# Attention's output projection in seven half products: where its weight sums are kept, in which order the products run, and how far ahead the factors are loaded

## The chip, the core and the metric

The kernel runs on one core of a Trainium2 chip. The core has five engines that run side by side, each with its own instruction queue in order: TensorE (PE, matmuls, with PEld for loading the stationary operand), VectorE (DVE), ScalarE (ACT), GpSimd (POOL) and SyncE (SP). SP issues nearly all plain loads from memory; POOL issues those that add to what already lies in the tile. Engines wait for each other on semaphores. The metric is the device time of one execution in microseconds, lower is better; the time before is the median of 3 runs, 1007.43 us (1006.94 to 1008.52).

## What is computed

A decoder trunk of two layers, one sequence of 512 tokens, width 1024, everything in float32. Layer 0 mixes tokens by causal pooling, layer 1 by attention with three groups of heads (windows of 128, 512 and 2048 with dilations 1, 4, 16). Both layers end in a SwiGLU block.

```python
for i in range(DEPTH):
    h = rmsnorm(x, norm_mix[i])
    if i % N_MIXERS == 0:
        y = pool_mixer(h, pool_w_in[j], pool_w_group[j], pool_scale[j], pool_w_out[j])
    else:
        y = attn_mixer(h, attn_w_qkv[j], attn_w_out[j])
    x = x + y
    h = rmsnorm(x, norm_ffn[i])
    x = x + swiglu(h, ffn_w_gate[i], ffn_w_up[i], ffn_w_down[i])
return rmsnorm(x, norm_final)
```

The last step of `attn_mixer` is what matters here. Each head's output is scaled by its group's share, the 16 heads are put side by side (`merged`, 512 x 1024), and the result is multiplied by `attn_w_out` (1024 x 1024):

```python
merged = jnp.concatenate(
    [o_g * (N_ATTN_GROUPS * alpha[:, :, g]).astype(o_g.dtype)[:, :, None, None] for g, o_g in enumerate(outs)],
    axis=2,
).reshape(B, S, D_ATTN)
return jnp.einsum('bse,ed->bsd', merged, w_out)
```

## The kernel before

**Precision.** Every float32 matrix is split in two parts, `hi` (a cast to fp32r) and `lo` (the rest, `x - hi`), and a product is three matmuls: hi*hi, hi*lo, lo*hi. A weight tile of 128 x 1024 thus costs one cast on ACT (line 179) and one subtraction on DVE (line 183).

**The stream of weights.** All weight tiles stand in one list, `queue`, in the order of use. `weights(i)` (line 157) does three things: it loads tiles up to `load_ahead` places on (an item's own `ahead` overrides it), it splits loaded tiles up to `split_ahead` places on, and it hands out item `i`. Raw tiles come from the pool `wraw` (5), split ones from the ring `wspl` (5 pairs) or, for items with `"pool": "b"`, from a second pool that is open only for a while. `held` says how many ring tiles are in use elsewhere. An item with `"sums"` takes its raw tile from `pools["s"]`, and loading stops at such an item while that pool isn't open (line 161). An item with `"cast_behind"` has its cast put behind a named instruction on ACT.

**Order.** PE runs in program order. On the other engines a planner orders the instructions before the run by priority, its own costs and due times; `tc.high_priority(URGENT)` puts a block ahead, `tc.issue_after(ins)` puts it behind an instruction on the same engine. At run time each engine keeps the planned order.

**Seven half products.** Attention's output projection multiplies the merged matrix by the weight in the manner of Strassen and Winograd: with both cut in quarters, seven products take the place of eight. `SEVEN_OUT = (False, True)` uses it for attention only; layer 0 runs the plain `out_projection`. Each product has a left operand (a quarter or a sum of quarters of the merged matrix, split to hi and lo by `Left`) and a right operand, two weight items z = 0, 1 (`enqueue_seven`, line 207). Products 0, 3 and 6 use a plain quarter of the weight; 4 adds a second block by DMA; product 1's item is a sum in a tile of its own (the `sraw` of the trace: a base by SP, a second block added by POOL). Products 2 and 5 use that same tile after one more block each is added to it (`loads`, line 188), which can only be issued after the split of the item before. The products accumulate in three pairs of PSUM banks: `accs = {0: p, 1: r, 2: p, 3: q, 4: p, 5: r, 6: p}`; after each, `flush` adds the banks into the residual stream `x` on DVE.

The order before is 0, 1, 2, 5, 4, 3, 6. `seven_projection` (line 554) runs it: 24 matmuls a product (line 571), and between products the left splits (`left.behind`), the squares and gains of the norm, and before product 6 the transposes of the first two blocks of rows (`turned_rows`). `left.reserve` takes a ring tile for the left operand `u4`.

**What comes ahead of it.** After the scores and the value projection, the group shares go through a small DMA to memory (`far`) and come back as factors, spread over the partitions (`weights_of`, line 1434, two POOL DMAs each). `merged(t)` (line 1521) makes two heads' output on PE in one of 4 PSUM banks (`mm`), and DVE multiplies it by factor `t` into a raw tile (lines 1538 and 1542). Five factors are loaded ahead, into `LB0` to `LB2` and the halves of `even_rows`; the other three follow as tiles come free. Along with it `Left.first` and `Left.second` make the first left operands. The raw tiles are parts of `pT`, the transposed scores.

`angles` holds the cosines and sines of the rotary embedding, `odd_rows` rows of the norm; `masks` the score masks, in the tile that the norm's `gain` takes later.

Of the kernel before, what the change touches and what calls it, by code (L numbers as in the profile page):

```python
# [17 lines left out]
P = 128  # L18
# [52 lines left out]
SEVEN = (0, 1, 2, 5, 4, 3, 6)  # L71
# [7 lines left out]
def trunk_kernel(ctx: ExitStack, tc: tile.TileContext, x_in, xT, gam, gains, consts, ident_d, w0, wT, w1, wv, w_down, out):  # L79
# [49 lines left out]
    def load(i):  # L129
# [3 lines left out]
        if item.get("sums"):  # L133
            raw = pools["s"].tile([P, 1024], F32, name="sraw")
        else:
            raw = (pools["v"] if item["kind"] == "v" else wraw).tile([P, 1024], F32, name="vraw" if item["kind"] == "v" else "wraw")
# [20 lines left out]
    def weights(i, split_ahead=4, load_ahead=5, held=0):  # L157

        load_ahead = queue[i].get("ahead", load_ahead)
        for n in range(loaded["w"], min(len(queue), i + load_ahead)):  # L160
# [5 lines left out]
        load_sums()  # L166
        while len(ready) < min(loaded["w"], i + split_ahead):
# [36 lines left out]
    j_in.append([enqueue(w0[i], (2, S)) for i in range(4, 8)])  # L204
    w_out, wo = (rows_of(wT[i]) for i in range(2))

    def enqueue_seven(w, order, then=None):
# [295 lines left out]
    class Left:  # L503
# [6 lines left out]
        def split(self, u, src, ks=(slice(0, 4),)):  # L510
            hi, lo = self.places[u]
            for k in ks:
                split(hi[:, k, :], lo[:, k, :], src[:, k, :])
# [33 lines left out]
        def reserve(self):  # L547

            if 4 not in self.places:
                self.places[4] = [  # L550
                    wspl.tile([P, 1024], F32R, name=name).rearrange("p (k s) -> p k s", k=4) for name in ("whi", "wlo")
                ]

    def seven_projection(js, left, norm, shift, p, r, q, tps, after_first, keep):
# [8 lines left out]
        def products(i, ws, ts=range(2)):  # L563
            hi, lo = left.places[(0, 1, 2, 3, 6, 5, 4)[i]]
            places = [(z, t, c) for z in range(2) for t in ts for c in range(2)]
# [16 lines left out]
        def product(i):  # L582
            products(i, operands(i))
# [16 lines left out]
        product(5)  # L600
# [24 lines left out]
    with ExitStack() as pctx:  # L625
# [4 lines left out]
        if SEVEN_OUT[0]:  # L630
            raw = [pm.tile([P, 4, S], F32, name=f"raw{i}") for i in range(2)]
            spare_sum = pm.tile([P, 4, 256], F32, name="spare_sum")
        p_hi, p_lo = (pm.tile([P, NC, S], F32R, name=name) for name in ("p_hi", "p_lo"))
# [53 lines left out]
        for k in range(2):  # L687
# [3 lines left out]
            if k == 0:  # L691
                nc.vector.tensor_sub(bands_lo, bands[:, :, :HEAD], bands_hi[:, k, :, :HEAD].bitcast(F32))
        v, s, r = (tmp.tile([P, 4], F32, name=name) for name in ("v4", "s4", "r4"))
# [36 lines left out]
        def group_products(half, banks):  # L730
            whi, wlo = weights(j_grp[half])
            for gg in range(2):
                g = 3 - (2 * half + gg)
                for m in range(2):
# [7 lines left out]
                    if SEVEN_OUT[0]:  # L742
                        with tc.high_priority(URGENT):
                            nc.scalar.activation(raw[half][:, 2 * gg + m, :], ps, AF.Copy, scale=sc)
# [6 lines left out]
                    )  # L751

# [19 lines left out]
        if SEVEN_OUT[0]:  # L772
            pools["s"] = open_pool("pools", 2)
            p, r = ([mm.tile() for _ in range(2)] for _ in range(2))

            def after_first():
                group_products(1, early)
# [396 lines left out]
    with ExitStack() as actx:  # L1174
# [8 lines left out]
        angles = aw.tile([P, D], F32, name="angles", bufs=1)  # L1183
# [183 lines left out]

        ring = [ap.tile([P, S], F32, name=f"LB{g}") for g in range(3)]
# [133 lines left out]
        seven = SEVEN_OUT[1]  # L1502
        pools["b"] = actx.enter_context(tc.tile_pool(name="wob", bufs=3 if seven else 4, reuse_waits="tile"))
        if seven:
            pools["s"] = actx.enter_context(tc.tile_pool(name="wos", bufs=2, reuse_waits="tile"))
        two = mp.tile([P, D], F32, name="even_rows")
        of_heads = [weights_of(t, to) for t, to in enumerate(ring + [two[:, cs] for cs in COLS])]
        m_hi, m_lo = h_hi, h_lo
        if seven:
# [5 lines left out]
            places.update({6: places[0], 3: places[1]})  # L1515
            left = Left(raw, fours(flat_p, 8 * S, 256), places)
# [4 lines left out]
        def merged(t):  # L1521
# [14 lines left out]
            with tc.high_priority(URGENT):  # L1536
                if t < 3:
                    nc.vector.tensor_mul(o, ps, of_heads.pop(0))
                    of_heads.append(weights_of(5 + t, ring[t]))
# [104 lines left out]
```

## Time and profile before

| | |
|---|---|
| median of 3 runs | 1007.43 us |
| the profiled execution | 1007.74 us |
| its span | 1006.0 us |
| PE busy | 975.3 us, 97% |
| DVE busy | 800.7 us, 80% |
| ACT busy | 583.6 us, 58% |
| POOL busy | 134.8 us, 13% |
| read from memory | 165.09 MB |

The span is the time from the first to the last instruction; the profiled execution's own time is 1.7 us longer. A line of a group or of a timeline names the engine, the line of the kernel, the operation, the tile written and the tiles read, and, in brackets, how long the engine was idle before it and who ended that. A line of waits has the total, the number and the longest. A line of windows gives the busy time (and the number of instructions) of PE, PEld, DVE, ACT and POOL in a stretch, then the granted clock of TensorE (1.00 is full), the share of the DMA engines, and GB/s. Where a helper makes all instructions of a kind, they have one line, so the names of the tiles tell them apart: `sraw` is product 1's sum, `bhi` and `blo` are splits in the second pool, `sc`, `mm` and `tp` are PSUM banks.

### The profile page before, as it was taken

How to read it: one execution, taken by the hardware profiler on the slowest of the kernel's cores; microseconds unless marked ns; L12 is line 12 of the kernel's file. 1: busy time of each engine (PE TensorE's matmuls, PEld its weight loads, DVE VectorE, ACT ScalarE, POOL GpSimd, SP SyncE). 2: the span in 40 equal slices, each digit the busy share in tenths (PEclk: the TensorE clock that was granted, in tenths of full speed). 3: DMA queues.
4: the chain of work that ended last, by engine and by line, in shares of the span. 5: the costliest groups of instructions: out<-in, count | busy, mean ns of one | idle time of the engine just before them, and what ended most of it. 6: DMA issues, size and time to landing. Idle time of an engine off the chain costs nothing. (4 is left out here: it accounts for less than half of the span.)

```text
span 1006.0 us, 15591 instructions
## 1 busy us (share of the span) xinstructions
PE 975.3 (97%) x6004; PEld 863.5 (86%) x6004; DVE 800.7 (80%) x1099; ACT 583.6 (58%) x909; POOL 134.8 (13%) x132
## 2 busy tenths in 40 slices
PE   9999999999999999999999986879999999999997
PEld 7888899988988998898888985669998898899886
DVE  6475799888897888688976528789989788888877
ACT  5573666656755767474534614567655566566655
POOL 0002010111012101102121141011101101111110
PEclk9999999999999999999999997889999999999999
DMA  8557276589469866652222295586747966887652
GB/s 323 185 175 181 46 216 169 140 208 239 125 175 253 211 179 147 159 194 91 84 61 66 85 234 103 152 190 186 190 126 202 246 166 148 225 240 174 157 123 118
DMA packets 82186, 168.24 MB, mean 167 GB/s; under 512 B 6256, under 2 KB 6640, under 8 KB 82112
## 3 DMA queue, kind: packets, MB, share of 16 engines
q1 hardware_dynamic: 59088, 123.09, 37.2%
q0 software_dynamic: 22736, 43.89, 25.5%
q8 instruction: 47, 0.77, 0.3%
q10 hardware_dynamic: 288, 0.27, 0.1%
q14 instruction: 27, 0.22, 0.1%
HBM read 165.09 MB, written 2.13 MB: 166 GB/s over the span
## 5 line engine op out<-in xcount | busy, mean ns | idle before, releaser
L183 DVE TENSOR_TENSOR wlo<-wraw,whi 128x1024 fp32r<-128x1024 f32 (+2 forms) x190 | 221.8, 1172 | 59.7 <-ACT whi L179 59.0
L179 ACT CAST whi<-wraw 128x1024 fp32r<-128x1024 f32 (+2 forms) x189 | 183.9, 979 | 129.9 <-PE pair L888 28.0
L179 ACT CAST whi<-vraw 128x1024 fp32r<-128x1024 f32 (+1 forms) x108 | 105.1, 979 | 120.4 <-DVE vraw L185 40.7
L183 DVE TENSOR_TENSOR wlo<-vraw,whi 128x1024 fp32r<-128x1024 f32 (+1 forms) x108 | 121.5, 1133 | 47.1 <-ACT whi L179 47.0
L888 PE MATMUL pair<-h,whi 128*128 128x512 f32 (+1 forms) x640 | 143.2, 349 | 0.0
L888 PEld LDWEIGHTS pair<-h,whi 128*128 128x128 f32 x640 | 109.1, 189 | 13.4
L888 PE MATMUL pair<-t,whi 128*128 128x512 f32 (+1 forms) x512 | 110.6, 337 | 0.0
L1032 PE MATMUL pair<-whi,u_hi 128*128 128x512 f32 (+1 forms) x284 | 109.9, 387 | 0.0
L1032 PE MATMUL pair<-wlo,u_hi 128*128 128x512 f32 (+1 forms) x284 | 109.9, 387 | 0.0
L1032 PE MATMUL pair<-whi,u_lo 128*128 128x512 f32 (+1 forms) x284 | 109.7, 386 | 0.0
L888 PEld LDWEIGHTS pair<-t,whi 128*128 128x128 f32 x512 | 86.0, 190 | 8.4
L888 PE MATMUL pair<-h,wlo 128*128 128x256 f32 x512 | 89.2, 281 | 0.0
L888 PEld LDWEIGHTS pair<-h,wlo 128*128 128x128 f32 x512 | 76.1, 188 | 4.2
L144 POOL DMA_DIRECT2D wraw<-w x22 | 26.6, 1209 | 388.0 <-DMA wraw<-w 112.7
L185 DVE TENSOR_TENSOR vraw<-vraw,wraw 128x1024 f32<-128x1024 f32 (+1 forms) x66 | 75.2, 1139 | 0.6
L888 PE MATMUL pair<-t,wlo 128*128 128x256 f32 x384 | 71.9, 282 | 0.0
L299 PE MATMUL mm<-h,whi 128*128 128x512 f32 (+1 forms) x176 | 64.3, 365 | 0.0
L301 PE MATMUL mm<-h,wlo 128*128 128x512 f32 (+1 forms) x176 | 63.4, 360 | 0.0
L300 PE MATMUL mm<-h,whi 128*128 128x512 f32 (+1 forms) x176 | 63.4, 360 | 0.0
L1032 PEld LDWEIGHTS pair<-whi,u_lo 128*128 128x128 f32 x284 | 53.3, 188 | 10.7
L1032 PEld LDWEIGHTS pair<-whi,u_hi 128*128 128x128 f32 x284 | 53.4, 188 | 10.4
L1032 PEld LDWEIGHTS pair<-wlo,u_hi 128*128 128x128 f32 x284 | 53.4, 188 | 10.3
(399 smaller groups left out, 2053.3 us busy)
## 6 DMA issues: line engine op xcount, KB each, us to landing
wraw<-w SPq DMA_DIRECT2D x116, 512.0 KB, 4.4
wraw<-w_down SPq DMA_DIRECT2D x32, 512.0 KB, 4.1
vraw<-w SPq DMA_DIRECT2D x22, 512.0 KB, 4.6
wraw<-w POOLq DMA_DIRECT2D x22, 512.0 KB, 7.6
vraw<-w POOLq DMA_DIRECT2D x22, 512.0 KB, 8.9
wraw<-wT SPq DMA_DIRECT2D x16, 512.0 KB, 4.7
vraw<-w_down POOLq DMA_DIRECT2D x12, 512.0 KB, 6.6
wraw<-w_down SPq DMA_DIRECT2D x24, 256.0 KB, 3.2
```

What stands on the lines that cost most here:

```text
L144: nc.gpsimd.dma_start(dst, more, accum_op=ALU.add)
L179: nc.scalar.copy(hi[:, :n], raw[:, :n])
L183: nc.vector.tensor_sub(lo[:, :n], raw[:, :n], hi[:, :n].bitcast(F32))
L185: nc.vector.tensor_add(raws[into][:, :n], raws[into][:, :n], raws[more][:, :n])
L299: nc.tensor.matmul(ps, lhsT=whi, rhs=xhi, start=first, stop=False, **kw)
L300: nc.tensor.matmul(ps, lhsT=whi, rhs=xlo, start=False, stop=False, **kw)
L301: nc.tensor.matmul(ps, lhsT=wlo, rhs=xhi, start=False, stop=last, **kw)
L888: mat = lambda o, w, m, **kw: nc.tensor.matmul(o, lhsT=w, rhs=m, skip_group_check=True, **kw)
L1032: nc.tensor.matmul(acc(t), lhsT=u, rhs=w, start=first, stop=n == len(places) - 1, skip_group_check=True)
```

## The change

Eight edits, most of them in the attention layer:

1. The sums' raw tiles: instead of a pool of two tiles that opens after the scores, `pools["s"]` gives `odd_rows` and `angles`, and it is there from the end of the loop over queries and keys. `angles` moves to the pool that lives through the whole layer.
2. Only products from the third in the order on put their second half in pool `b`; both halves of products 0 and 1 take ring tiles.
3. The order is 0, 1, 2, 4, 5, 3, 6.
4. Product 2's two casts are tied behind the casts of the left operands 1 and 2.
5. `Left.behind`: the splits for 5, 6, 3 and 4 leave the urgent block and stand behind other products; `u4` has its own tile (`reserve` is gone).
6. In `seven_projection` the squares and gains stand elsewhere, product 5's weights are asked for ahead of them, and product 6 is cut so that the transposes stand between its first and second half of block 0.
7. Six factors ahead: `masks` takes the sixth.
8. In layer 0, the last input weight has `ahead` 8, and the second group's weights are asked for with `split_ahead` 1.

The parts under `SEVEN_OUT[0]` (sums and ties in the pooling layer) aren't run, as that flag is off.

```diff
-SEVEN = (0, 1, 2, 5, 4, 3, 6)
+SEVEN = (0, 1, 2, 4, 5, 3, 6)
...
-            raw = pools["s"].tile([P, 1024], F32, name="sraw")
+            raw = pools["s"]()
...
+    def load_until(end):
+
+        for n in range(loaded["w"], min(len(queue), end)):
             if queue[n].get("sums") and "s" not in pools:
                 break
             if queue[n]["kind"] == "w":
                 load(n)
             loaded["w"] = n + 1
         load_sums()
...
-    j_in.append([enqueue(w0[i], (2, S)) for i in range(4, 8)])
+    j_in.append([enqueue(w0[i], (2, S), **({"ahead": 8} if i == 7 else {})) for i in range(4, 8)])
...
-                item = dict(kind="w" if src else "sum", shape=(2, S), rows=True, ahead=8, **({"pool": "b"} if z else {}))
+                item = dict(kind="w" if src else "sum", shape=(2, S), rows=True, ahead=8, **({"pool": "b"} if z and i > 1 else {}))
...
-            with tc.high_priority(URGENT):
-                if i is None:
+            if i is None:
+                with tc.high_priority(URGENT):
                     self.next_sum(FIRST)
                     self.split(2, self.spare)
-                    self.split(5, more[:, :, FIRST])
-                    nc.vector.tensor_sub(t[:, :, FIRST], more[:, :, FIRST], t[:, :, FIRST])
-                elif i == 0:
-                    self.split(6, t[:, :, FIRST])
-                elif i == 1:
-                    self.split(3, more[:, :, SECOND])
-                    self.next_sum(SECOND)
-                elif i == 4:
-                    self.split(4, self.spare)
+            elif i == 0:
+                nc.vector.tensor_sub(t[:, :, FIRST], more[:, :, FIRST], t[:, :, FIRST])
+                self.split(6, t[:, :, FIRST])
+            elif i == 1:
+                self.split(5, more[:, :, FIRST])
+                self.next_sum(SECOND)
+            elif i == 2:
+                self.split(3, more[:, :, SECOND])
+                self.split(4, self.spare)
...
-            return [weights(j, split_ahead=6, held=z + (i in (4, 3, 6))) for z, j in enumerate(js[i])]
+            return [weights(j, split_ahead=6, held=z) for z, j in enumerate(js[i])]
...
         product(1)
         product(2)
-        product(5)
+        product(4)
+        ws = operands(5)
+        for b in range(2):
+            norm.square(b, 1)
+            norm.gained(b, 1)
+        product(5, ws)
         for b in range(2):
             norm.square(b, 0)
             norm.gained(b, 0)
-        left.reserve()
-        product(4)
-        for b in range(2):
-            norm.square(b, 1)
-            norm.gained(b, 1)
             norm.prepare(b)
         product(3)
         for t in range(2):
             norm.square(2 + t, 0, q[t])
-        rests = turned_rows(norm, shift, list(enumerate(tps())))
         ws = operands(6)
-        rests()
+        products(6, ws, (0,), (0,))
+        turned_rows(norm, shift, list(enumerate(tps())))()
+        products(6, ws, (0,), (1,))
         for t in range(2):
+            if t:
+                products(6, ws, (1,))
             norm.gained(2 + t, 0)
-            products(6, ws, (t,))
             flush(6, t)
...
-            whi, wlo = weights(j_grp[half])
+            whi, wlo = weights(j_grp[half], 1 if half else 4)
...
-        angles = aw.tile([P, D], F32, name="angles", bufs=1)
+        seven = SEVEN_OUT[1]
+        angles = (ap if seven else aw).tile([P, D], F32, name="angles", bufs=1)
...
+        if seven:
+            free = [odd_rows, angles]
+            pools["s"] = lambda: free.pop(0)
...
-        if seven:
-            pools["s"] = actx.enter_context(tc.tile_pool(name="wos", bufs=2, reuse_waits="tile"))
-        two = mp.tile([P, D], F32, name="even_rows")
-        of_heads = [weights_of(t, to) for t, to in enumerate(ring + [two[:, cs] for cs in COLS])]
+        two = mp.tile([P, D], F32, name="even_rows")
+        factors = ring + [two[:, cs] for cs in COLS]
+        if seven:
+            factors.append(masks[:, :S])
+        of_heads = [weights_of(t, to) for t, to in enumerate(factors)]
...
+            places[4] = [mp.tile([P, 4, 256], F32R, name=name) for name in ("u4_hi", "u4_lo")]
...
-                    of_heads.append(weights_of(5 + t, ring[t]))
+                    if len(factors) + t < 8:
+                        of_heads.append(weights_of(len(factors) + t, ring[t]))
...
                     elif t == 4:
                         left.second()
+                        queue[j_wo[2][0]]["cast_behind"] = left.cast.ins
                     elif t == 7:
                         left.behind(None)
+                        queue[j_wo[2][1]]["cast_behind"] = left.cast.ins
```

More of the change, by code (lines that the diff above doesn't have):

```diff
@@ L155, in load_sums @@
                 done.append(i)
-    def weights(i, split_ahead=4, load_ahead=5, held=0):
-        load_ahead = queue[i].get("ahead", load_ahead)
-        for n in range(loaded["w"], min(len(queue), i + load_ahead)):
+    def load_until(end):
+        for n in range(loaded["w"], min(len(queue), end)):
             if queue[n].get("sums") and "s" not in pools:
@@ L166, in weights @@
         load_sums()
+    def weights(i, split_ahead=4, load_ahead=5, held=0):
+        load_ahead = queue[i].get("ahead", load_ahead)
+        load_until(i + load_ahead)
         while len(ready) < min(loaded["w"], i + split_ahead):
@@ L512, in split @@
             for k in ks:
-                split(hi[:, k, :], lo[:, k, :], src[:, k, :])
+                self.cast = split(hi[:, k, :], lo[:, k, :], src[:, k, :])[0]
         def first(self, k):
@@ L532, in behind @@
             t, more = self.raw
-            with tc.high_priority(URGENT):
-                if i is None:
+            if i is None:
+                with tc.high_priority(URGENT):
                     self.next_sum(FIRST)
                     self.split(2, self.spare)
-                    self.split(5, more[:, :, FIRST])
-                    nc.vector.tensor_sub(t[:, :, FIRST], more[:, :, FIRST], t[:, :, FIRST])
-                elif i == 0:
-                    self.split(6, t[:, :, FIRST])
-                elif i == 1:
-                    self.split(3, more[:, :, SECOND])
-                    self.next_sum(SECOND)
-                elif i == 4:
-                    self.split(4, self.spare)
[L547 to L552, printed above, removed]
+            elif i == 0:
[7 more added lines that the diff above has]
+                self.split(4, self.spare)
     def seven_projection(js, left, norm, shift, p, r, q, tps, after_first, keep):
@@ L560, in operands, with products @@
         def operands(i):
-            return [weights(j, split_ahead=6, held=z + (i in (4, 3, 6))) for z, j in enumerate(js[i])]
-        def products(i, ws, ts=range(2)):
+            return [weights(j, split_ahead=6, held=z) for z, j in enumerate(js[i])]
+        def products(i, ws, ts=range(2), zs=range(2)):
             hi, lo = left.places[(0, 1, 2, 3, 6, 5, 4)[i]]
-            places = [(z, t, c) for z in range(2) for t in ts for c in range(2)]
+            places = [(z, t, c) for z in zs for t in ts for c in range(2)]
             for z, t, c in places:
@@ L580, in flush, with product @@
                     nc.vector.tensor_sub(at, at, accs[i][t])
-        def product(i):
-            products(i, operands(i))
+        def product(i, ws=None):
+            products(i, ws or operands(i))
             for t in range(2):
@@ L632, in trunk_kernel @@
             spare_sum = pm.tile([P, 4, 256], F32, name="spare_sum")
+            sums = [pm.tile([P, 1024], F32, name=f"sum{i}") for i in range(2)]
         p_hi, p_lo = (pm.tile([P, NC, S], F32R, name=name) for name in ("p_hi", "p_lo"))
@@ L692, in trunk_kernel @@
                 nc.vector.tensor_sub(bands_lo, bands[:, :, :HEAD], bands_hi[:, k, :, :HEAD].bitcast(F32))
+        if SEVEN_OUT[0]:
+            pools["s"] = lambda: sums.pop(0)
+            load_until(j_out[1][-1] + 1)
         v, s, r = (tmp.tile([P, 4], F32, name=name) for name in ("v4", "s4", "r4"))
@@ L743, in group_products @@
                         with tc.high_priority(URGENT):
-                            nc.scalar.activation(raw[half][:, 2 * gg + m, :], ps, AF.Copy, scale=sc)
+                            made = nc.scalar.activation(raw[half][:, 2 * gg + m, :], ps, AF.Copy, scale=sc)
                             if half == 0 and m == 1:
@@ L751, in group_products @@
                     )
+            return SEVEN_OUT[0] and made
         quarters = lambda t: t.rearrange("p a b -> p (a b)").rearrange("p (u k s) -> p u k s", u=4, k=4)
@@ L772, in trunk_kernel @@
         if SEVEN_OUT[0]:
-            pools["s"] = open_pool("pools", 2)
             p, r = ([mm.tile() for _ in range(2)] for _ in range(2))
             def after_first():
-                group_products(1, early)
+                made = group_products(1, early)
+                for i in (2, 5):
+                    for j in j_out[i]:
+                        queue[j]["cast_behind"] = made.ins
                 left.second()
```

1 line of the change is left out of this document (removed).

## The prediction

> **What bounds the kernel now.** I read the page first, then the windows over the attention layer's end, who waited for whom there, and last the order of time on ACT, DVE, POOL and SP.
>
> ```profile
> span 1006.0 us, 15591 instructions
> ...
> PE 975.3 (97%) x6004; PEld 863.5 (86%) x6004; DVE 800.7 (80%) x1099; ACT 583.6 (58%) x909; POOL 134.8 (13%) x132
> ```
>
> TensorE is the bound: idle for 1006.0 - 975.3 = 30.7 us in all, and no edit here removes a matmul. So a gain can only come from that idle time and the slow clock behind it. Most lies in one place (windows: PE, PEld, DVE, ACT, POOL busy with counts, then PE clock, DMA share, GB/s):
>
> ```profile
> core 0: us, PE busy (x) PEld busy (x) DVE busy (x) ACT busy (x) POOL busy (x), PEclk, DMA share, GB/s
> 594.07:601.57 7.50, 7.43 (x132) 7.18 (x132) 3.13 (x5) 0.34 (x2) 6.69 (x11) 1.00 0.79 236
> 601.57:609.92 8.35, 0.00 (x1) 0.00 (x1) 2.48 (x4) 2.33 (x3) 3.00 (x5) 0.73 0.94 205
> 609.92:625.91 15.99, 15.99 (x81) 13.15 (x81) 15.35 (x16) 6.26 (x8) 2.80 (x4) 0.82 0.48 83
> 625.91:631.39 5.48, 0.00 (x1) 0.00 (x0) 4.97 (x7) 1.90 (x2) 0.00 (x0) 0.81 0.00 0
> 631.39:668.00 36.61, 33.17 (x151) 25.93 (x151) 28.19 (x46) 22.69 (x35) 6.06 (x5) 0.89 0.73 184
> 680.05:720.35 40.30, 40.30 (x339) 40.09 (x337) 40.28 (x55) 26.66 (x38) 4.84 (x4) 1.00 0.71 183
> 594.07:722.30 128.23, 105.97 (x764) 95.24 (x765) 106.13 (x148) 69.87 (x102) 24.59 (x29) 0.91 0.68 166
> PE mm L1532 <- DVE pT L1538: 8.4, 1, 8.4
> PE sc L571 <- DVE wlo L183: 5.5, 1, 5.5
> PE pair L914 <- ACT keep L966: 2.0, 1, 2.0
> PE mm L401 <- ACT even_rows L387: 1.9, 1, 1.9
> ```
>
> Between the merged heads' first matmul (594.07) and the FFN's wait that ends at 722.30, PE idles 128.23 - 105.97 = 22.3 us; 8.4 and 5.5 of it are two single waits. The same rows warn: DVE is busy 15.35 of 15.99, 4.97 of 5.48 and 40.28 of 40.30 us. Wherever PE stops waiting, DVE is nearly full.
>
> The first wait is a blocked head of a queue:
>
> ```profile
> 584.69 1.07 SPq L142 DMA_DIRECT2D sraw<-wT  x2
> 593.01 3.14 POOL L1438 DMA_DIRECT2D LB<-far  x6 [7.96 <-DMA far<-ropea]
> 598.32 2.54 POOL L144 DMA_DIRECT2D sraw<-wT  x2
> 606.36 1.04 ACT L179 CAST whi<-sraw 128x1024 fp32r<-128x1024 f32 x1 [11.94 <-DMA sraw<-wT]
> 607.44 1.23 DVE L183 TENSOR_TENSOR wlo<-sraw,whi 128x1024 fp32r<-128x1024 f32 x1 [8.46 <-ACT whi L179]
> 609.18 0.68 DVE L1538 TENSOR_TENSOR pT<-mm,LB 128x512 f32<-128x512 f32 x1
> ```
>
> Product 1's weight sum has its base at 584.69, but its adding DMA stands on POOL behind the factors (598.32), so ACT casts it only at 606.36. DVE stands in order before its rest (8.46 us idle), and behind that is the third multiply, which frees the PSUM bank that PE waits for.
>
> The second wait has two parts:
>
> ```profile
> 630.12 1.22 DVE L183 TENSOR_TENSOR wlo<-sraw,whi 128x1024 fp32r<-128x1024 f32 x1
> 631.26 1.22 DVE L183 TENSOR_TENSOR blo<-sraw,bhi 128x1024 fp32r<-128x1024 f32 x1
> 631.96 1.22 POOL L188 DMA_DIRECT2D sraw<-wT  x1 [10.79 <-DVE wlo L183]
> 637.82 1.06 ACT L179 CAST whi<-sraw 128x1024 fp32r<-128x1024 f32 x1 [10.01 <-DMA sraw<-wT]
> 638.91 1.22 DVE L183 TENSOR_TENSOR wlo<-sraw,whi 128x1024 fp32r<-128x1024 f32 x1 [6.44 <-ACT whi L179]
> ```
>
> PE waits to 631.39 for product 2's rest (630.12), which DVE did last of a full stretch. Then DVE idles 6.44 us: product 5 needs that same sum plus one more DMA (issued 631.96, landed 637.82, 5.9 us), its cast stands first on ACT, and product 4's casts, whose data came long before, stand behind it.
>
> And the end of the stretch is DVE's too:
>
> ```profile
> 720.72 1.04 ACT L179 CAST whi<-vraw 128x1024 fp32r<-128x1024 f32 x1 [3.82 <-DVE vraw L185]
> ```
>
> PE's wait on ACT's `keep` (2.0 us) ends at 722.30 because ACT stood 3.82 us behind a DVE addition, with DVE busy throughout. DVE's backlog reaches that far.
>
> **The change, part by part.**
>
> *Sums in early tiles.* The two product 1 sums get `odd_rows` and `angles`. Removed: the wait for the pool that opens after the scores.
>
> ```profile
> L393 PE MATMUL sc<-ident,odd_rows x8: 271/272/273, 447.2 to 448.0; 128*128 128x128 f32 x8
> L1204 POOL TENSOR_TENSOR ropeb<-ropeb,angles x16: 1272/1292/1304, 454.9 to 544.3; 128x512 f32<-128x512 f32 x16
> ```
>
> Their last readers before are at 448.0 and 544.3 + 1.3 = 545.6, 39 us ahead of 584.69. Two SP loads and two POOL adds (2.54 us) move before the far write; POOL was busy 134.8 us of 1006, which hides them. With the sum there, casts and rests of both halves of product 1 run when the ring gives a tile, and DVE's 8.46 us go. The two rests cost 1.14 us each (630.12 to 631.26), 2.28 us, and fall into DVE's idle time before the merge:
>
> ```profile
> 593.80 1.23 DVE L183 TENSOR_TENSOR blo<-wraw,bhi 128x1024 fp32r<-128x1024 f32 x1 [9.56 <-ACT bhi L179]
> 584.17 0.88 POOL L1432 DMA_DIRECT2D far<-ropea  x1
> DVE pT L1538 <- DMA LB<-far: 1.8, 2, 1.2
> ```
>
> The write of the factors to `far` (584.17, landed by 593.01) loses two 512 KB neighbours on the DMA engines. DVE waited 1.8 us for factors, so an earlier landing is worth 0 to 1.8; I take 0, because no row shows how much of the 8.8 us the neighbours made.
>
> *Two products in the ring, ties, order 2-4-5.* Both halves of products 0 and 1 take ring tiles as the value projection frees them. Product 2's casts are tied on ACT behind the left splits that PE needs earlier (behind a tied cast stand ACT's later casts, whose operands PE needs later still), and the splits for 5 and 6 leave the urgent block, so product 2's rests no longer come last. Product 4 now lies between 2 and 5: one product (5.44 us below) more for the 5.9 us DMA, and its casts no longer stand behind the late one. So the 6.44 us go. If that cover fails, some of it returns.
>
> *The new wait.* Products 2 and 4 both accumulate in `p`, now one right after the other: PE's first matmul of 4 waits until DVE has added product 2 from that bank. Behind that matmul stand all of PE's later ones; DVE itself isn't held.
>
> ```profile
> L571 PE MATMUL mm<-whi,h x16: 389/389/502, 620.1 to 642.6; 128*128 128x512 f32 x16
> 623.73 1.27 DVE L578 TENSOR_TENSOR x<-sc,x 128x512 f32<-128x512 f32 x2
> ```
>
> Product 1 began at 620.1, so product 0 had ended, and its flush began 3.6 us later: the wait is 0 to 3.6 us of PE. Product by product DVE keeps working meanwhile, so in DVE's sum it is 0.
>
> Likewise ACT's squares of block 1 write `odd_rows`, where product 5's sum now lies, and wait for its rest; PE needs that rest at the same moment for product 5, so this adds nothing.
>
> *Six factors ahead.* `masks` holds the sixth, so two POOL DMAs (3.14/6 = 0.52 us each) come before the first multiply instead of behind it; this shares the 0 to 1.8 above, and I take 0. The norm's gain load shares that tile and must now wait on SP for the sixth multiply:
>
> ```profile
> gain<-gains SPq DMA_DIRECT2D x4, 512.0 KB, 4.0
> ```
>
> Its 4.0 us lie beside the four products (21.8 us) that precede its first reader. If SP held the later weight loads behind it, they would come late by up to the same 4.0.
>
> *Tile for u4, split 4 after product 2, norms and transposes inside product 6.* Same instructions, placed earlier; six matmuls (6 x 0.227 = 1.4 us) lie before the transposes that waited 1.9. 0 to -1.4; I take 0 because DVE feeds that chain.
>
> *Layer 0.* `ahead` 8 loads up to three weights earlier and the second group's weights split only themselves; PE waits nowhere there but for 1.5 us in its first 20 us, which hides both (uncovered, one 1.14 us rest for the second; the first is a rival below). The pool's seven-product path is switched off.
>
> **The sum** against the profiled execution, 1007.74 us (its span 1006.0; the median of the runs is 1007.43). Two bounds:
>
> ```profile
> 646.28:651.72 5.44, 5.44 (x25) 4.50 (x24) 5.44 (x10) 5.13 (x8) 0.00 (x0) 1.00 0.82 295
> ```
>
> PE alone: a product is 24 matmuls in 5.44 us at full clock (0.227 each). From 601.57: 32 merged matmuls at 7.43/132 = 0.056 are 1.8; seven products 38.1; 32 transposes, priced like the merged ones, 1.8. Sum 41.7, so 643.3 instead of 668.0: 25 us.
>
> DVE: from 594.07 to 722.30 it is idle 128.23 - 106.13 = 22.1 us. 8.46 + 6.44 = 14.90 go, and 2.28 of work moves ahead: 17.2. The other 7.2 us (factors, norm chains) I leave. Since DVE is full to 722 and PE waits for it there, the smaller one decides: 1007.7 - 17.2 = 990.5; behind 722.30 no PE wait is listed, so it passes to the end. On the runs' median that is 990.2; I say 990.
>
> [...] In this trace the clock drops behind short waits too:
>
> ```profile
> 660.00:664.00 4.00, 3.77 (x24) 3.15 (x25) 4.00 (x8) 2.71 (x7) 2.19 (x2) 0.57 1.06 274
> ```
>
> Only 1.9 and 0.3 us of waiting lie just ahead, and 0.43 x 4.0 = 1.7 us of clock are lost. [...]
>
> **Rivals.**
>
> *PE alone decides.* If DVE's backlog is prefetch that isn't needed in time, 1007.7 - 25 = 983. For: DVE has slack after 722. Against: 40.28 of 40.30, and ACT's 3.82 us behind DVE.
>
> *Half of it.* Only the first wait goes (8.4, and the slow clock behind it, 15.99 x 0.18 = 2.9), while the second is replaced by the new wait and by DVE, full with the same splits: 1007.7 - 11 = 997; with 3.6 + 1.7 against it, up to 1002. For: the second wait's first half was DVE's order, not a DMA. Against: that order is what the ties alter.
>
> *The change doesn't do it.* If the adding DMAs still stand behind the factors on POOL, or DVE's order still puts a waiting rest ahead of the third multiply, nothing moves: 1007.5.
>
> *Slower, in layer 0.* SP's queue is in order:
>
> ```profile
> 22.32 2.41 SPq L683 DMA_DIRECT2D x<-x_in  x4
> 33.33 0.33 SPq L689 DMA_DIRECT2D spare<-consts  x1
> 53.63 1.22 DVE L183 TENSOR_TENSOR wlo<-wraw,whi 128x1024 fp32r<-128x1024 f32 x1 [3.23 <-ACT whi L179]
> ```
>
> With `ahead` 8 the third extra load takes the raw tile that is free when the rest at 53.63 ends (54.85). If it stands before the bands' load, that one moves from 33.33 to 54.85, and the windows' matmuls, which need the bands, wait 21.5 us: 1007.7 + 21.5 - 17.2 = 1012. It decides once the held load stands ahead of the bands and attention saves less than 21.5. Against: SP took `x_in` at 22.32 ahead of weights with earlier places, so loads without a free tile aren't put first.
>
> **Chances.** Forecast 990 (985 to 996): 0.45. PE alone: 0.15. Half (996 to 1005): 0.20. No change: 0.08. Slower: 0.12. A difference of 0.2%, 2 us, is about what can be told from none. Faster 0.80, same 0.08, slower 0.12. The range, 981 to 1006, takes in the PE bound with its unknowns and the half case, and leaves out the slower one and most of no change.
>
> **What would show it.** Right: adding DMAs for product 1's sums well before 584; no DVE idle over 2 us between the second and third multiply; PE's waits of 8.4 and 5.5 gone; product 6's end near 645 to 651; DVE busy over 95% from 600 to 705, and a PE wait left in the FFN's start. Wrong: the FFN stretch passes without a wait (PE alone), a wait at the first matmul of product 4 over 2 us, or a hole at 39 to 55 us.

## The result, and the profile after

The changed kernel takes 1001.00 us (median of 4 runs, 1000.07 to 1003.43) against 1007.97 us (4 runs, 1006.94 to 1010.26): a ratio of 0.9931, 95% interval 0.9907 to 0.9956. It is faster by 7 us. The forecast was 990, so the direction was right and under half of the forecast's 17 us arrived. The profiled execution took 1000.07 us, its span is 998.3.

First the page of the changed kernel: the span, the engines' busy time, PE's busy tenths and the granted clock in 40 slices of 25 us.

```profile
span 998.3 us, 15594 instructions
...
PE 975.0 (98%) x6004; PEld 863.8 (87%) x6004; DVE 800.2 (80%) x1099; ACT 584.2 (59%) x909; POOL 135.2 (14%) x132
...
PE   9899999999999999999999999989899999999997
...
PEclk9889999999999999999999999999999999999999
```

The second and third slice, 25 to 75 us, now read 8 in the clock and the second reads 8 in PE. That is layer 0, where the prediction had the change cost nothing. The windows of the same trace (columns as in the prediction), and behind them who PE waited for (total, number, longest), say it in microseconds:

```profile
38.78:43.61 4.83, 0.00 (x2) 0.01 (x1) 2.03 (x9) 4.03 (x10) 0.00 (x0) 0.82 0.58 169
43.61:55.50 11.89, 11.89 (x45) 10.93 (x46) 5.90 (x9) 4.39 (x8) 0.00 (x0) 0.50 0.01 4
603.59:713.12 109.53, 98.75 (x765) 89.07 (x765) 102.48 (x144) 67.53 (x98) 20.25 (x25) 1.00 0.72 181
```

```profile
PE early L725 <- DVE u_lo L706: 4.8, 1, 4.8
...
PE pair L921 <- ACT keep L973: 3.1, 1, 3.1
PE sc L568 <- DVE x L575: 2.3, 1, 2.3
...
PE mm L1545 <- DVE pT L1551: 1.0, 1, 1.0
```

In the kernel before, PE had no idle time in the second of these windows, at full clock:

```profile
43.61:55.50 11.89, 11.89 (x64) 10.19 (x63) 3.25 (x5) 3.39 (x5) 0.00 (x0) 1.00 0.01 1
```

The third window is the one that the prediction's sum was made for: from the merged heads' first matmul to the end of the FFN's wait. It took 128.23 us before and takes 109.53 now: **18.7 us saved**, where 17.2 were forecast. The waits of 8.4 and 5.5 us are gone; the clock is 1.00 instead of 0.91.

But the merge now starts at 603.59 instead of 594.14: **9.45 us are lost ahead of it.** The first two windows hold them: a wait of 4.8 us for the windows' operands, and then 11.89 us at half clock (about 5.9 us of work lost). That makes 10.8, and 1.3 of it is won back elsewhere ahead of the merge: the run without `ahead` 8 below, which has no hole, starts its merge 1.0 us earlier than the kernel before. What wins it isn't known. To a fixed matmul of the FFN (736.65 before, 728.99 after; from there PE has 263.0 us left in every profile) the balance is 17.1 saved and 9.45 lost, 7.7 us, which is the difference of the two profiled executions, 1007.74 and 1000.07.

How the hole comes about stands in SP's order of time, and in one row of DVE's:

```profile
21.25 3.96 SPq L142 DMA_DIRECT2D wraw<-wT  x2
25.26 0.46 SPq L683 DMA_DIRECT2D x<-x_in  x1
30.28 0.37 SPq L142 DMA_DIRECT2D wraw<-wT  x1
30.70 1.41 SPq L683 DMA_DIRECT2D x<-x_in  x3
...
38.65 0.33 SPq L689 DMA_DIRECT2D spare<-consts  x1
```

```profile
29.03 1.23 DVE L187 TENSOR_TENSOR wlo<-wraw,whi 128x1024 fp32r<-128x1024 f32 x1 [4.22 <-ACT whi L183]
```

Before, the four loads of `x` went out together at 22.32. Now a weight load stands ahead of the first, held on SP until about 25, and a second one ahead of the other three, held until 30.28: it needs the raw tile that the rest of 29.03 + 1.23 = 30.26 sets free. Behind it wait three quarters of `x`: the second is issued at 30.70 instead of 22.83, and the last lands at 38.62 instead of 32.00. The bands (`spare`, 38.65 instead of 33.33) are late by way of `x`: the norm's squares of `x` use the same tile first, and the last of them ends at 38.63. The norm needs `x`, the windows' operand `u_lo` needs the norm, and PE needs `u_lo`.

In attention the sums behave as forecast, by POOL's order of time and by DVE's around the merge:

```profile
466.20 1.20 POOL L144 DMA_DIRECT2D odd_rows<-wT  x1 [11.67 <-DMA odd_rows<-wT]
560.54 1.21 POOL L144 DMA_DIRECT2D angles<-wT  x1 [4.70 <-DVE wlo L187]
```

```profile
601.25 1.22 DVE L187 TENSOR_TENSOR wlo<-angles,whi 128x1024 fp32r<-128x1024 f32 x1 [2.25 <-ACT whi L183]
...
609.10 0.69 DVE L1551 TENSOR_TENSOR pT<-mm,LB 128x512 f32<-128x512 f32 x1 [3.02 <-DMA LB<-far]
...
611.27 0.69 DVE L1551 TENSOR_TENSOR pT<-mm,LB 128x512 f32<-128x512 f32 x1
```

The adding DMAs are issued at 466 and 561, product 1's rests lie ahead of the merge, and between the second and third multiply DVE is never idle for more than 0.7 us. What is late next is the second factor: DVE waits 3.02 us for `LB`, PE 1.0.

### The profile page after: what moved, and what is told of

It is laid out like the page before. It is cut to its first block, busy times and chain, and to the rows that moved or that the text cites. A ratio compares the mean times of both kernels' runs of the same rounds, so it can differ in the third digit from the quotient of the medians.

```text
span 998.3 us, 15594 instructions
## 1 busy us (share of the span) xinstructions
PE 975.0 (98%) x6004; PEld 863.8 (87%) x6004; DVE 800.2 (80%) x1099; ACT 584.2 (59%) x909; POOL 135.2 (14%) x132
## 5 line engine op out<-in xcount | busy, mean ns | idle before, releaser
L1039 PEld LDWEIGHTS pair<-wlo,u_hi 128*128 128x128 f32 x284 | 53.4, 188 | 10.2
```

The lines of the kernel that those rows point to most:

```text
L1039: nc.tensor.matmul(acc(t), lhsT=u, rhs=w, start=first, stop=n == len(places) - 1, skip_group_check=True)
```

## The experiments

In each diff only the lines of the edit are shown. All ratios are to the kernel before, with their 95% intervals.

### Layer 0: the eighth place ahead

My theory after the result: `ahead` 8 on the last input weight makes the hole and nothing else in layer 0 does (A). Against it: the clock, the second group's `split_ahead` 1, or a DMA pattern that moved with the attention edits (B).

**The change without it.**

```diff
-    j_in.append([enqueue(w0[i], (2, S), **({"ahead": 8} if i == 7 else {})) for i in range(4, 8)])
+    j_in.append([enqueue(w0[i], (2, S)) for i in range(4, 8)])
```

> The changed kernel with the ahead of 8 on layer 0's last input weight taken back, everything else kept. Theory A (the extra loads stand ahead of x_in on SP and hold it until their raw tiles are free; that is the whole of the missing gain): the wait of 4.8 us at the windows' matmuls and the slow clock behind it go, the merged heads start at 594 instead of 603.6, and the time is 1001 - 9.5 = 991.5. Theory B (the 9.5 us come from something else in layer 0, such as the second group's split_ahead of 1): 1001 as before. Theory C (the attention layer saves less than its trace says, for instance because its stretch is measured from a late start): between, 995 to 999.

Measured: 992.42 us (5 runs, 990.04 to 995.73), ratio 0.9850 (0.9828 to 0.9872), as theory A had it. SP's order of time has `x` in one go again, and the merge starts at 593.11:

```profile
20.99 2.17 SPq L683 DMA_DIRECT2D x<-x_in  x4
```

**The kernel before with it alone.** The same line, in the other direction, and nothing else.

> The kernel before with the ahead of 8 alone. Theory A: 1008 + 9.5 = 1017.5, with a wait of about 4.8 us before the first windows' matmul and about 13.7 us of half clock behind it. Theory B: 1008.

Measured: 1019.05 us (4 runs, 1017.15 to 1021.80), ratio 1.0115 (1.0091 to 1.0139). Its SP queue and PE's wait repeat the pattern of the changed kernel:

```profile
25.12 0.46 SPq L683 DMA_DIRECT2D x<-x_in  x1
30.13 0.37 SPq L142 DMA_DIRECT2D wraw<-wT  x1
30.55 1.41 SPq L683 DMA_DIRECT2D x<-x_in  x3
```

```profile
PE early L722 <- DVE u_lo L703: 4.3, 1, 4.3
```

By the medians it costs 12 us alone (from 1007.20) and taking it away returns 9. By the start of the merge, which leaves attention out, the two agree: 10.15 us (604.29 against 594.14) and 10.48 (603.59 against 593.11). A holds in both directions.

**Six places instead of eight** (one extra load instead of three).

```diff
-**({"ahead": 8} if i == 7 else {})
+**({"ahead": 6} if i == 7 else {})
```

> The changed kernel with ahead 6 in place of 8: one extra load, the one whose raw tile is free at 25.4 us, and not the one whose tile is free only at 30.3. Theory A (what costs is how long SP is held ahead of x_in): x_in is issued from about 25 us on in one go instead of three of four at 30.7, the windows wait 0 to 2.5 us, and the time is 992 to 996. Rival (the extra traffic slows x_in, in proportion to the loads): a third of 9.5 us remains, and x_in's landing grows, not its issue time.

One run: 994.91 us. SP's order of time in it:

```profile
20.93 4.21 SPq L142 DMA_DIRECT2D wraw<-wT  x2
25.18 1.89 SPq L683 DMA_DIRECT2D x<-x_in  x4
```

One extra load already holds `x` back by four microseconds, but all four quarters then go together, and each lands no later after its issue than without the load (4.9 to 7.8 us against 6.3 to 8.4; the changed kernel has 4.6 to 6.9, the kernel before 5.9 to 8.1). So it is the issue that is late, and no slowing by the traffic shows: theory A's mechanism. PE waits only 0.6 and 0.5 us at the windows. Even so the merge starts at 598.23, 5.1 us later than without extra loads, because half clock follows:

```profile
39.12:42.53 3.41, 2.73 (x19) 2.31 (x19) 3.22 (x7) 3.04 (x6) 0.00 (x0) 1.00 0.06 24
42.53:49.36 6.83, 6.83 (x27) 6.21 (x26) 2.74 (x5) 1.76 (x3) 0.00 (x0) 0.50 0.01 4
```

6.83 us at half clock are 3.4 us of work. So one held load costs about half of what two do (10.48), and more by the clock than by waiting. The time alone, 994.91, wouldn't decide: the rival's third of 9.5 us gives nearly the same.

**The second group's splits as before**, on top of the first run.

```diff
-            whi, wlo = weights(j_grp[half], 1 if half else 4)
+            whi, wlo = weights(j_grp[half])
```

> The changed kernel without the ahead of 8 and with the second group's split_ahead back at its default of 4. Theory A: as the kernel without the ahead, 991.5, within 1.5 us. Theory B: 6 to 10 us faster than that kernel.

Measured: 988.88 us (4 runs, 986.04 to 994.47), ratio 0.9826 (0.9789 to 0.9863). The merge starts at 594.02, so layer 0 isn't shorter, and the interval overlaps that of the first run. `split_ahead` 1 is worth nothing that can be told. This and the first run are both faster than the two kernels compared here.

### Attention: one edit taken back, or made alone

For these runs a split of the stretch helps. It runs from the merge's first matmul to the fixed matmul of the FFN; the windows view gives it for each profile (first number: the length, second: PE busy). In turn the kernel before, the changed one, the run without `ahead` 8, and the run with the splits as before:

```profile
594.14:736.65 142.51, 120.32 (x876) 109.24 (x877) 118.06 (x160) 78.67 (x111) 26.62 (x30) 0.92 0.69 169
```

```profile
603.59:728.99 125.40, 114.62 (x877) 104.59 (x877) 114.43 (x156) 76.40 (x108) 22.35 (x27) 0.99 0.72 180
```

```profile
593.11:718.95 125.84, 115.69 (x877) 105.44 (x877) 114.53 (x156) 76.60 (x108) 22.10 (x26) 0.97 0.71 179
```

```profile
594.02:716.79 122.77, 112.83 (x877) 102.94 (x877) 114.36 (x156) 76.49 (x108) 21.95 (x26) 1.00 0.73 184
```

The last had full clock throughout, so 112.8 us is what the matmuls of the stretch take. What PE's busy time has above that is the clock; the length minus the busy time is waiting. Before: 22.2 us of waiting and 7.5 of clock. After: 10.8 and 1.8. **So of the 17.1 us that attention gained, 11.4 are waits and 5.7 the clock behind them.**

| kernel | waiting | clock | stretch |
|---|---|---|---|
| before | 22.2 | 7.5 | 142.5 |
| changed | 10.8 | 1.8 | 125.4 |
| changed without `ahead` 8 | 10.2 | 2.9 | 125.8 |
| and splits as before | 9.9 | 0 | 122.8 |
| early sums alone (wait ahead of the merge included) | 13.1 | 4.5 | 130.5 |
| order 5, 4 | 16.2 | 5.2 | 134.2 |
| five factors | 12.6 | 7.0 | 132.4 |
| no ties | 13.9 | 5.5 | 132.2 |
| four rests on POOL | 16.4 | 5.1 | 134.3 |
| four rests made twice | 11.4 | 2.1 | 126.4 |
| product 2 by blocks | 11.6 | 1.5 | 125.9 |

**The early sums alone**, on the kernel before.

```diff
-            raw = pools["s"].tile([P, 1024], F32, name="sraw")
+            raw = pools["s"]()
...
-        angles = aw.tile([P, D], F32, name="angles", bufs=1)
+        angles = ap.tile([P, D], F32, name="angles", bufs=1)
...
+        free = [odd_rows, angles]
+        pools["s"] = lambda: free.pop(0)
...
-        if seven:
-            pools["s"] = actx.enter_context(tc.tile_pool(name="wos", bufs=2, reuse_waits="tile"))
```

> The kernel before with one edit alone: product 1's sums in odd_rows and angles, loaded as soon as these are free. Theory A (the first wait is DVE's blocked queue behind that sum, 8.4 us and 2.9 us of clock; the second wait has its own cause, the order of DVE's splits): 996 to 998, with a wait of 3 us or more left at products 2 or 5. Rival (one cause for both, the chain of sums starts too late): both waits go and the time is 991.

Measured: 994.26 us (4 runs, 992.04 to 996.51), ratio 0.9863 (0.9842 to 0.9885). Both waits are gone with this one edit, not only the first. In their place PE waits ahead of the merge (its list of waits), and ACT's order of time shows for what:

```profile
PE mm L1532 <- ACT v L1495: 5.4, 1, 5.4
```

```profile
597.42 1.04 ACT L179 CAST whi<-odd_rows 128x1024 fp32r<-128x1024 f32 x1 [12.04 <-DMA odd_rows<-wT]
598.37 0.74 ACT L1495 COPY v<-mm 128x320 f32<-128x320 f32 x2
```

Product 2's cast stands first on ACT, 12 us idle for its data, and the copies of `v` that the merge needs stand behind it. Even with this wait the interval overlaps that of the change without `ahead` 8: most of what attention gains comes from this one edit (13.7 of 14.8 us by the medians, 12.0 of 16.7 by the table). With the other edits the new wait is gone. The tie of that cast (edit 4) would be enough for it, but the run without the ties, below, doesn't have the wait either, and which edit removes it isn't shown. The next runs take single edits away, all from the change without `ahead` 8.

**The old order**: 5 before 4, and the norm's squares where they were.

```diff
-SEVEN = (0, 1, 2, 4, 5, 3, 6)
+SEVEN = (0, 1, 2, 5, 4, 3, 6)
```

> The changed kernel without the ahead of 8, with the order 0, 1, 2, 5, 4, 3, 6 of before. Theory A (the new order costs 2.3 us of waiting for bank p, and buys a product's time for product 5's sum): the wait at bank p goes, a wait of 2 to 6 us for product 5's weights comes, and the stretch from the merged heads to the FFN's wait is 0 to 4 us longer. Rival (the order buys nothing, since the sums are early now): no wait takes its place; PE is 2.3 us ahead at product 6, the time is the same because DVE sets the end, or up to 2.3 us less.

Measured: 997.97 us (4 runs, 995.61 to 1000.58), ratio 0.9899 (0.9873 to 0.9926). The wait for bank `p` is gone, and among PE's waits there is a longer one:

```profile
PE mm L568 <- DVE h L427: 5.5, 1, 5.5
```

It is the left operand of product 5, whose rest now comes too late (626.73): on DVE it stands behind the rest of product 5's second weight half, whose sum in `angles` was late.

```profile
624.98 1.23 DVE L187 TENSOR_TENSOR blo<-angles,bhi 128x1024 fp32r<-128x1024 f32 x1 [2.55 <-ACT bhi L183]
```

This interval lies just above that of the run without `ahead` 8: with the other edits in place the new order saves some 6 us of waiting, and the bank's wait is its smaller price. It isn't shown that the order is worth that by itself. Edit 5 puts the split for product 5 behind product 1, which suits the new order and is kept in this run; the early sums alone, with the order and the splits of before, have no such wait.

**Five factors ahead** instead of six.

```diff
-        if seven:
-            factors.append(masks[:, :S])
```

> The changed kernel without the ahead of 8, with five factors ahead instead of six. Theory A (factors wait at most 1.8 us): as the kernel without the ahead within 1.5 us. Rival: the sixth multiply waits for a factor that is loaded late, DVE idles 2 us or more before it, and the time is 2 to 4 us longer.

Measured: 996.75 us (4 runs, 990.84 to 997.75), ratio 0.9875 (0.9844 to 0.9907). DVE doesn't idle before the sixth multiply, as the rival had it; it waits 4.27 us for the second factor, 2.67 in the run without `ahead` 8.

**Without the ties.**

```diff
-                        queue[j_wo[2][0]]["cast_behind"] = left.cast.ins
...
-                        queue[j_wo[2][1]]["cast_behind"] = left.cast.ins
```

> The changed kernel without the ahead of 8 and without the two ties of product 2's casts. Theory A (the ties keep ACT's queue from being blocked by a cast whose DMA is late): ACT waits 4 us or more for product 2's sum ahead of the left splits, and the time is 3 to 8 us longer. Rival (the sums are early enough, or the planner puts the casts there anyway): within 1.5 us of the kernel without the ahead.

Measured: 995.83 us (4 runs, 995.01 to 996.93), ratio 0.9879 (0.9864 to 0.9894). ACT does wait for product 2's sum ahead of the left splits, as theory A said, but behind the copies of `v`:

```profile
597.86 1.05 ACT L183 CAST whi<-odd_rows 128x1024 fp32r<-128x1024 f32 x1 [5.50 <-DMA odd_rows<-wT]
```

The intervals of these last two runs overlap that of the run that they are taken from. By the table each adds 2.4 to 3.7 us of waiting and 2.6 to 4.1 of clock, in waits that lie all over the stretch; without ties the longest is at the transposes:

```profile
PE mm L405 <- ACT even_rows L391: 4.0, 1, 4.0
```

By the medians the sixth factor would be worth 4.3 us and the ties 3.4, where the prediction had 0; that they are worth anything the intervals don't show.

### Does VectorE's load set the end?

The prediction's sum went by DVE: full to 722, so a microsecond less of idle time or work on DVE is one less in all. Two runs test that, one with less work on DVE and one with more.

**Four rests on POOL** (left operands 3 to 6).

```diff
-                self.cast = split(hi[:, k, :], lo[:, k, :], src[:, k, :])[0]
+                self.cast = split(hi[:, k, :], lo[:, k, :], src[:, k, :], nc.gpsimd if u in (3, 4, 5, 6) else None)[0]
```

> The changed kernel without the ahead of 8, with the rests (x - hi) of the four left operands 3, 4, 5 and 6 made on POOL instead of DVE. Theory A (DVE's load sets the stretch from the merged heads to the FFN's wait): 4 x 1.14 = 4.5 us leave DVE, and the time falls by 3 to 4.5 us below the kernel without the ahead. Rival (what is left are single dependencies, such as bank p and the norm's chain): within 1.5 us; POOL, slower for such an operation, may even hold product 4 or 5 by 2 to 3 us.

Measured: 998.07 us (4 runs, 996.94 to 1000.04), ratio 0.9906 (0.9883 to 0.9930): slower than without it. But it isn't the test that it was meant to be, as POOL's order of time shows, and DVE's behind it:

```profile
611.13 3.27 POOL L427 TENSOR_TENSOR h<-pT,h 128x1024 fp32r<-128x1024 f32 x1 [7.25 <-ACT h L426]
...
623.18 2.70 POOL L427 TENSOR_TENSOR h<-pT,h 128x1024 fp32r<-128x1024 f32 x1 [1.34 <-ACT h L426]
```

```profile
612.65 2.84 DVE L542 TENSOR_TENSOR pT<-pT 128x1024 f32<-128x1024 f32 x1
...
623.60 3.36 DVE L187 TENSOR_TENSOR wlo<-odd_rows,whi 128x1024 fp32r<-128x1024 f32 x1
```

The same two instructions of DVE take 1.23 us each where these rests stay on DVE (run without `ahead` 8):

```profile
612.28 1.23 DVE L542 TENSOR_TENSOR pT<-pT 128x1024 f32<-128x1024 f32 x1
...
620.89 1.23 DVE L187 TENSOR_TENSOR wlo<-odd_rows,whi 128x1024 fp32r<-128x1024 f32 x1
```

DVE lost four instructions and got no freer: busy 117.71 us in the stretch, against 114.53, and PE's wait at bank `p` grew from 2.3 to 5.8 us. So this run says nothing of a lighter DVE.

**The same rests made twice on DVE**: the second computes the same values again.

```diff
+                if u in (3, 4, 5, 6):
+                    nc.vector.tensor_sub(lo[:, k, :], src[:, k, :], hi[:, k, :].bitcast(F32))
```

> The changed kernel without the ahead of 8, with the same four rests made twice on DVE, the second time writing the same values again. Theory A: 4.5 us more DVE work, 3 to 5 us longer. Rival: within 1.5 us.

Measured: 990.22 us (4 runs, 989.17 to 991.58), ratio 0.9826 (0.9808 to 0.9844), no slower than without the extra work, which is 4 x 1.13 = 4.5 us of DVE. Its stretch in the windows view:

```profile
592.99:719.34 126.35, 114.94 (x878) 103.83 (x878) 117.28 (x159) 75.75 (x108) 24.26 (x29) 0.99 0.72 181
```

DVE is busier by 2.8 us in the records, and the stretch is 0.5 us longer: DVE's idle time in it went from 11.3 to 9.1 us. So it had time to give, and a microsecond of work on it isn't one of the stretch. The planner also put DVE's instructions in another order here: the FFN's wait of 3.1 us isn't there, and waits of 1.5 and 2.2 us at product 3 are. What the same work would cost in a fixed order isn't shown; that PE waits for which instruction DVE has in hand, and not for how many, is what fits.

### The new wait at bank p

**Product 2 block by block**, with the splits as before: the first block of rows is done and added to `x` before the second begins.

```diff
-        product(2)
+        ws = operands(2)
+        for t in range(2):
+            products(2, ws, (t,))
+            flush(2, t)
+        left.behind(2)
```

> This is the changed kernel without the eighth place ahead and with the second group's splits as before (as in the run with both undone, 988.9 us), and product 2 runs its first block of rows to the end and adds it to x before its second block; the matmuls are the same. Theory A (the wait at product 4's first matmul, 2.2 us in that run, is the bank p that product 2's first block still holds: its addition starts 1.4 us behind the product's end, behind three weight rests of 1.13 us on DVE): block 0 ends 12 matmuls earlier, about 618.6 instead of 621.4, its addition goes ahead of those rests, and the wait falls to what product 4's own rests need: under 1.2 us. The stretch from the merge's start to the end of the last wait in the next block gets shorter by 1.0 to 2.2 us, and the time is 986.5 to 988, if the clock's windows are alike. Theory B (product 4 waits for its weights' rests as much as for the bank): the wait is the same 2 us with another releaser, and the time is 988 to 990. A time over 992 would say that the two additions put ahead hold up a rest that PE needs sooner.

Measured: 990.05 us (5 runs, 988.54 to 991.97), ratio 0.9823 (0.9797 to 0.9849). PE's waits say that the one at bank `p` is cut in two and not shorter, and DVE's order of time why:

```profile
PE sc L568 <- DVE x L575: 2.2, 2, 1.1
```

```profile
618.19 1.21 DVE L187 TENSOR_TENSOR wlo<-wraw,whi 128x1024 fp32r<-128x1024 f32 x1
619.33 1.21 DVE L187 TENSOR_TENSOR blo<-wraw,bhi 128x1024 fp32r<-128x1024 f32 x1
620.46 0.67 DVE L575 TENSOR_TENSOR x<-sc,x 128x512 f32<-128x512 f32 x1
```

Theory A said that the addition would go ahead of the rests. It doesn't: the two rests of product 4's own weights still stand ahead of it, and the bank is added out at 621.13, as the last of three instructions that product 4 needs. The total stays 2.2 us and the time, 990.05, is at the upper end of theory B's (988 to 990): moving the addition alone would make a rest the last one. PE's wait at the transposes, 3.0 us here and 1.0 in the run that it is taken from, was not expected by either.

## Why the prediction was right, and where it was wrong

**The step that failed** is the one on layer 0: "PE waits nowhere there but for 1.5 us in its first 20 us, which hides both". It counted PE's waits as they were, and not what the extra loads stand in front of on SP. They cost 9.45 us. This term alone turns 990 into 1000: 1007.7 - 17.2 + 9.45 = 1000.0, against 1000.07 measured in the profiled execution.

**The rival that named it** had the mechanism (a load without a tile, at the head of SP's queue, ahead of the windows' operands) and the place ("a hole at 39 to 55 us": it is at 38.8 to 43.6, with half clock to 55.5). It had the wrong load: the second extra one, whose tile comes free at 30.26, not the third at 54.85; the operand that came late was `x`, and the bands only by way of it; and so its price was 21.5 instead of 9.45, and its sign wrong: attention's gain was larger. The argument that kept it at 0.12, "loads without a free tile aren't put first", is refuted by the rows at 30.28 and 30.70; only the third extra load was put behind `x` and the bands. It was drawn from one issue of the kernel before, where the weight loads behind `x` also come later in the program.

**The attention sum** was 17.2 us and the measured gain 18.7 to the FFN's wait and 17.1 to the fixed matmul. Its steps: the sums' DMAs early, right; both single waits gone, right; product 6's end, 659.17, is 645 to 651 once the 9.45 us are taken off, right; DVE busy over 95% from 600 to 705, right (609.5 to 714.5 in the shifted trace, 101.85 of 105.00 us, 97%):

```profile
609.50:714.50 105.00, 94.22 (x670) 84.54 (x667) 101.85 (x143) 68.92 (x99) 15.98 (x16) 1.00 0.72 182
```

A wait left in the FFN's start, right (3.1 us). One of its signs of being wrong came as well, a wait over 2 us at product 4's first matmul (2.3), without harm to the sum. But **the reason given for the size fell.** DVE being full was taken as proof that it sets the end; with 4.5 us more work for DVE the end came 0.5 us later. In that stretch DVE's idle time fell by 15.05 us and its work by 3.65, where the sum had 14.90 and 2.28. But a stretch is always DVE's work plus its idle time, so this is bookkeeping of the same two waits, during which DVE stood still too, and no proof of what sets the end. What went on PE are two single waits, and the slow clock behind them. That a sum made for another cause came out at the right size is in part luck.

**Parts.** *Both waits by one edit*: the prediction gave 8.46 to the sums and 6.44 to ties and order together. The early sums alone remove both, and leave one of 5.4 us elsewhere; with the other edits that wait is gone, with or without the ties. *Bank p*: 0 to 3.6 us of PE was the bound, 2.3 came. *Six factors and ties at 0*: the profiles without them show 2.4 and 3.7 us more waiting, inside the spread of the time. *Factors*: a gain of 0 to 1.8 us from fewer neighbours was taken as 0; DVE's wait for the second one is now 3.02 us, so nothing was won. *Half of it* gave the right time, 996 to 1005, for a wrong cause: the second wait didn't come back.

**The clock.** The prediction had seen the clock drop behind 1.9 us of waiting (0.57 between 660 and 664), and in the half case it took up to 1.7 us of clock for the new wait. For bank p that wait of 2.3 us cost no clock in the changed kernel (1.00 from 55.5 to 714.3), and one of 2.3 us did in the run with the rests made twice. What the profiles show of both cases stands in the last section.

## What to carry to other kernels

A load that is asked for earlier is free only if its tile is (here loads without a free tile cost 9.45 us): on a queue in order, look for the row that frees the tile and list everything that stands behind it, with the first reader of each. An engine that is busy for 97% of a stretch doesn't bound it by that (here 4.5 us more work for it moved the end by 0.5); give it more work, and see whether the end moves. When an edit takes a wait away, count the slow clock behind it as part of the wait, here a third of the gain (5.7 of 17.1 us).

## What the hardware showed that was not expected

**In these profiles the clock went by windows of 3.41 us, and 2 us of waiting in one of them was enough.** In all 13, away from their ends, the half clock comes in pieces of 3.41, 6.83, 10.24 or 13.65 us, on one grid that doesn't follow the program. Between 560 and 975 us, 31 windows of that grid had PE idle for 1.97 us or more, and each was followed by half clock. Of those entered at full clock, none with 1.55 us or less was; between 1.6 and 1.92 us both occur. So a wait of 3.1 us cost clock or not by where it fell. The same wait, at the FFN's start, in the run without `ahead` 8 and in that with the splits as before:

```profile
699.53:702.94 3.41, 0.66 (x6) 0.45 (x4) 3.36 (x4) 1.27 (x2) 0.00 (x0) 1.00 0.12 19
702.94:706.35 3.41, 3.09 (x14) 3.10 (x15) 2.99 (x3) 2.85 (x4) 0.71 (x1) 0.50 0.86 290
```

```profile
697.59:701.00 3.41, 1.78 (x16) 1.57 (x14) 3.41 (x5) 0.35 (x2) 0.00 (x0) 1.00 0.00 1
701.00:704.41 3.41, 1.97 (x16) 1.97 (x17) 2.94 (x3) 3.41 (x5) 0.00 (x0) 1.00 0.65 181
```

In the first PE is idle for 2.75 us of one window, and the next has 0.50; in the second the wait lies on a boundary, 1.63 and 1.44 us, and the clock stays. In the kernel before, 1.98 us of waiting between 656.61 and 660.02 were followed by 0.50; in the changed kernel, 2.28 between 710.84 and 714.26 were, and 1.41 between 628.92 and 632.34 were not. All this is read from the profiles after the fact; no run was made to move a wait across the grid. It is also a good part of the spread: the five runs without `ahead` 8 have a mean granted clock of 0.996, 0.996, 0.994, 0.994 and 0.989 at 990.0, 991.8, 992.4, 992.6 and 995.7 us. That helps to explain why edits worth 2 us of waiting couldn't be told apart here.

Two pieces, both in layer 0, aren't explained by this. With `ahead` 8 the half clock lasts four windows (13.65 us) behind one wait of 4.8 us, though PE is busy for all 11.89 us after it. With 6 places it starts behind a window in which PE was idle for only 0.68 us. In the changed kernel the windows' narrow matmuls (128 x 144 at most) run from 43.61 to 51.62 without others between them, where the kernel before had 2.35 us of them in the 11.89; whether that bears on it, no run tells.

**A DVE instruction beside a subtraction on POOL took more than twice its time.** In the run with four rests on POOL, the four DVE instructions of 128 x 1024 that began while one of these rests ran took 2.84, 3.06, 3.36 and 2.82 us instead of 1.23. The one of 612.65 ends at 615.49, 1.09 us behind the POOL instruction's end at 614.40, and that of 623.60 at 626.96, 1.08 us behind 625.88; the other two end 1.08 us behind theirs. 1.1 us is about the time of such an instruction in a full row (1.13 from start to start). So they look as if they had begun their work when POOL ended: an estimate from these four pairs of rows.
